# A hybrid decoder layer on one core: other rates for the adaLN columns, pinned sums, later gates, and the mixer's silu by tanh

## The chip, the cores and the metric

The kernel runs on one core of one Trainium2 chip. The metric is the time of one execution in device microseconds (us). Before the change it is 1945.58 us, the median of three runs (1941.93 to 1946.73).

## The reference

One decoder layer of width 2048 for a sequence of 256 rows, in float32. Three residual branches follow one another, each behind an RMSNorm whose shift, scale and gate come from a conditioning vector (adaLN):

```python
cond = jax.nn.silu(c)
mod = cond @ ada_w[l] + ada_b[l]                      # 9 vectors of 2048
sh1, sc1, gt1, sh2, sc2, gt2, sh3, sc3, gt3 = jnp.split(mod, N_MOD, axis=-1)
x = x + 0.5 * gt1 * swiglu(ada_in(x, norm_g[l, 0], sh1, sc1), ...)       # 2048 -> 5632 -> 2048
x = x + gt2 * hybrid_mixer(ada_in(x, norm_g[l, 1], sh2, sc2), ...)
x = x + 0.5 * gt3 * swiglu(ada_in(x, norm_g[l, 2], sh3, sc3), ...)
```

The mixer projects once and runs two groups of eight heads of 128: forgetting attention (causal softmax with a decay from `log_sigmoid`), and a gated delta rule in chunks of 64. The lines of the second group that the change touches:

```python
qkv_g = jax.nn.silu(causal_dwconv(qkv_g, gdn_conv))          # 4 taps
g_log = -jnp.exp(gdn_A_log) * jax.nn.softplus(a_g + gdn_dt_bias)
beta  = jax.nn.sigmoid(b_g)
vb    = v * beta[..., None]
t_inv = triangular_solve(eye + lower, eye, ...)              # 64 x 64 blocks
o_g   = rmsnorm(o_g, gdn_out_norm) * jax.nn.silu(z)
```

## The kernel before

**Weights as one stream.** All matrices together are 5392 tiles of 128 x 128, used in an order fixed at build time, in 674 blocks of 8 tiles. For each block SyncE's queue issues one DMA of 512 KB (`wraw`, L125), ScalarE rounds it to a reduced float32 format (`whi`, L128) and VectorE subtracts to get the rest (`wlo`, L140; below "the split"). TensorE multiplies both parts. There are four buffers of each (a fifth `wraw` is in use in some stretches), so a weight DMA can go when the split four blocks earlier is done. The whole layer is one pass over this stream. By blocks: the first FFN's gate and up products 0 to 112 for its first 28 hidden groups, a first down product 112 to 168, gate and up for the rest 168 to 232 (the "second gate-up"), the second down product 232 to 264; the mixer's projections 264 to 378 and its output projection 378 to 410; the second FFN 410 to 674.

**Columns.** The nine adaLN vectors are computed as 144 columns of 128 values, 16 to a vector. A column takes a DMA of 1 MB (`adat`, L262) and one fused multiply-and-sum of 128 x 2048 on VectorE (L266). `RATE` says how many columns a block starts, from which block on. A sum is issued on VectorE in one of two ways: while `W.late` is set, it is owed and comes behind a split two blocks later (`BEHIND`, `settle`); otherwise it goes into the queue wherever the scheduler puts it. `ada_need` computes columns at once that a residual or norm needs and that aren't there yet. Before, `W.late` is set from the mixer on.

**The mixer's chains.** Projections (steps K, Z, V, F, G of `ORDER`: keys, z rows, values, forgetting heads, gated heads) feed generator chains: gates, decays, keys and solve in the chain "k", and one chain each for gated heads, forgetting heads and outputs. A clock advances by `TILE_US` with each weight tile, and a chain goes on when its last `yield` of so many microseconds has passed; so `yield` sets where in the weight stream the next piece of a chain is placed. `gates` transposes the gate rows (`pcol`, L845), computes softplus and sigmoid on VectorE as a row of small operations on 128 x 48 (L855 to L869), and multiplies by triangles (`prow`, L878). `solve` inverts 16 x 16 blocks for four heads at a time, in 15 dependent steps (L1015, L1016), and moves them through DRAM by DMA (`ld`, `lt`); its result is multiplied into U0 (L1029). Head rows come back from DRAM broadcast (`rowd`, L904 and L929). `conv_silu` takes a projection from PSUM (L955), applies four taps (L959 on ScalarE, L961 on VectorE) and a silu (L962). `gdn` runs a gated head: it transposes q and v (`pvq`, L1056), scales v by beta (`vb`, L1086), and so on. L1204 is the softmax exponential of a forgetting head, `ppt` (L1209) the transpose behind it.

**What sets the order.** Each engine works through its own queue in order. A scheduler writes these queues from the program; `issue_after` holds an instruction back until a given other one is written, of the same queue or another. ScalarE's activations come in sets of functions; the compiler puts an `ACT_TABLE_LOAD` ahead of an activation whose set isn't the loaded one.

Of the kernel before, what the change touches and what calls it, by code (L numbers as in the profile page):

```python
# [12 lines left out]
AF = mybir.ActivationFunctionType  # L13
ALU = mybir.AluOpType
# [18 lines left out]
GR = 24  # L33
NEG = -1e30

RATE = ((0, 0.5), (28, 0.25), (33, 0.5), (49, 0.25), (56, 0.5), (66, 0.2), (90, 0.0), (112, 0.5), (168, 0.45), (232, 0.26), (264, 0.0), (288, 0.295), (384, 0.0), (424, 0.16))
N_BIG, N_GDN = 3, 3
N_FIRST = 2
AHEAD = 4
# [4 lines left out]
LATER = 8  # L44
SLOTS = (3, 11)
BEHIND = 2

HA = 128 + 16
HS = 4 * HA
# [44 lines left out]
class Stream:  # L94


    def __init__(self, nc, w, raw, hi, lo):
        self.nc, self.w, self.raw, self.hi, self.lo = nc, w, raw, hi, lo
        self.order = []
        self.more = None  # L100
        self.h = self.l = self.last = None
        self.owed, self.side, self.quiet = 0.0, lambda: None, False
        self.tc, self.hold, self.held = None, None, []
        self.first = []
        self.lead = None
        self.late, self.owing = False, []

    def settle(self, upto=N_TILES):

# [21 lines left out]
    def next(self, mat, k, n, width=1):  # L131
        i = len(self.order)
        if i % WB == 0:
            nc = self.nc
            b = i // WB
            r, lo = self.first.pop(0) if self.first else self.block(b)
            self.l = lo.tile([P, WB * P], F32R, name="wlo")
            pace = [r_ for r_ in RATE if r_[0] <= b][-1][1]
            with self.behind():
                lo_ = nc.vector.tensor_tensor(self.l, r, self.h.bitcast(F32), ALU.subtract)  # L140
            with self.tc.issue_after(lo_.ins):
                self.settle(b - BEHIND)
            self.split = lo_.ins
            self.owed += 0.0 if self.quiet else pace
            while self.owed >= 1.0:
                self.owed -= 1.0
                self.side()
        for d in range(width):
            self.order.append((mat, k, n, width, d))
        o = (i % WB) * P  # L150
        h, l = self.h[:, o : o + width * P], self.l[:, o : o + width * P]
        return (h, l) if width == 1 else (woven(h), woven(l))
# [3 lines left out]
def layer_kernel(ctx: ExitStack, tc: tile.TileContext, xrow, c, adaw, cols, cst, w, out, order, dbg=None):  # L156
# [597 lines left out]
    def mixer():  # L754
# [76 lines left out]
        def gates(ps):  # L831
# [6 lines left out]
            coef = tiny.tile([P, GR + PAD["hid"]], F32, name="coef", bufs=1)[:, :GR]  # L838
            tc.keep_in_program_order(A.activation(coef, L("alog"), AF.Exp))
            V.tensor_scalar(coef, coef, -1.0, None, ALU.mult)  # L840
            yield 4.0
            pc = psf("pcol")
            pcv = pc[:, : 2 * GR].rearrange("p (t r) -> p t r", t=2)
            for t in range(2):
# [102 lines left out]
        uz = m1p.tile([P, P], F32, name="uz")  # L947
        for t_ in Tms + [Ub, vz, uz]:
            G.memset(t_, 0.0)

        def conv_silu(ps, n, dst, early=None):
            cp, cv = pt("cp"), pt("cv")
            tap = lambda s: L("conv", 4 * n + s, 1)
            if early is None:
                A.copy(runs(cp), turns(ps))  # L955
            else:
                s = early.scaled(cp, ps)
                A.activation(cp, cp, AF.Identity, bias=s)
            A.activation(cv, cp, AF.Copy, scale=tap(3))  # L959
            for d in range(1, 4):  # L960
                V.scalar_tensor_tensor(cv[:, d:], cp[:, : T - d], tap(3 - d), cv[:, d:], ALU.mult, ALU.add)  # L961
            A.activation(dst, cv, AF.Silu)  # L962

        kk = {}

# [23 lines left out]
        def solve(half):  # L989


            hs4, n = slice(4 * half, 4 * half + 4), 2 * NH // 2
            ht = slice(n * half, n * half + n)
            V.tensor_tensor(rb2[:, :, hs4], nbeg[:, :, hs4], r2[:, :, hs4], ALU.mult)
            rk = rsqrt(ssk[:, :, hs4], [P, 2, 4], "k")
            V.tensor_tensor(rkb[:, :, hs4], rk, colS[:, :, 4, hs4], ALU.mult)
            Lh = Ln[:, hs4].rearrange("p h t j -> p (h t) j")
            yield 4.0
            for b in range(8):
                r = slice(16 * b, 16 * b + 16)  # L1000
                with tc.issue_after(W.last):
                    nc.sync.dma_start(ld[ht, b].rearrange("n (r c) -> r n c", r=16), Lh[r, :, r])
                if b % 2:
                    yield 1.4
            yield 3.0
            B = slice(0, 8 * n)
            blk, xt_, pr = (x[B, j] for j in range(4, 7))
            with tc.issue_after(W.last):
                nc.sync.dma_start(blk, ld[ht].rearrange("n b e -> (n b) e"))
            yield 6.0  # L1010
            G.memset(xt_, 0.0)
            G.memset(xt_[:, 0:256:17], 1.0)
            bv, xv, pv = (t_.rearrange("p (i j) -> p i j", i=16) for t_ in (blk, xt_, pr))
            for i in range(1, 16):
                V.tensor_tensor(pv[:, :i, :i], xv[:, :i, :i], bv[:, i, :i].unsqueeze(1).to_broadcast([8 * n, i, i]), ALU.mult)  # L1015
                V.tensor_reduce(xv[:, :i, i], pv[:, :i, :i], mybir.AxisListType.X, ALU.add)  # L1016
                if i % 3 == 0:
                    yield 1.2
            yield 8.0
            with tc.issue_after(W.last):  # L1020
                nc.sync.dma_start(lt[ht].rearrange("n b e -> (n b) e"), xt_)
            yield 3.0
            U = x[:, 7, :P].rearrange("p (n i) -> p n i", n=n)
            with tc.issue_after(W.last):
                nc.sync.dma_start(U, lt[ht].rearrange("n b (q i) -> (b q) n i", q=16))
            yield 5.0
            for q in range(2):
                with tc.issue_after(W.split):
                    V.tensor_tensor(  # L1029
                        U0[:, hs4].rearrange("p h t (b i) -> p (h t) b i", b=4)[:, 4 * q : 4 * q + 4],  # L1030
                        U[:, 4 * q : 4 * q + 4].unsqueeze(2).to_broadcast([P, 4, 4, 16]),
                        C("blk").unsqueeze(1).unsqueeze(3).to_broadcast([P, 4, 4, 16]), ALU.mult)
            if half == 0:
                fetch_rows(1)
            yield 1.0
# [3 lines left out]
        def gdn(h):  # L1039
# [42 lines left out]
            for t in range(2):  # L1082
                sl = slice(t * P, (t + 1) * P)
                j2 = tmp.tile([P, P], BF16, name="j1")
                A.activation(j2, pv[:, T + t * P : T + (t + 1) * P], AF.Square, accum_out=ssq[:, t : t + 1])
                V.tensor_scalar(vb[:, t], pv[:, sl], rkb[:, t, h : h + 1], None, ALU.mult)  # L1086
                A.activation(kb[:, t], kT[:, 1, sl], AF.Copy, scale=rb2[:, t, h : h + 1])
                A.activation(kd[:, t], kT[:, 1, sl], AF.Copy, scale=colS[:, t, 3, h : h + 1])
            V.tensor_scalar(ssq, ssq, EPS, EPS * HD, ALU.add, ALU.mult)
# [156 lines left out]
        def step(kind, h):  # L1246
# [15 lines left out]
            elif kind == "Z":  # L1262
# [5 lines left out]
                pz = project_rows("z", h)  # L1268
                zss[h] = [spare(0), spare(2)] if h else [m1p.tile([P, 512], F32, name=f"zs{t}") for t in range(2)]
                for t in range(2):  # L1270
                    A.activation(zss[h][t], pz[t], AF.Silu)
            elif kind == "V":
                finish("k", NH if h else 0)
                pv = project_rows("vf", h)
# [10 lines left out]
                if h + 1 < NH:  # L1285
                    rowf[h + 1] = row_of(h + 1, 0, "f")

        W.late = True
        first = project([("gt", 0)] + [("qkv", NH + h) for h in range(3)], norm1)
        start("k", -1, gates(first[0]))  # L1290
        for h in range(3):
# [194 lines left out]
```

## Time and profile before

| | |
|---|---|
| median of three runs | 1945.58 us (1941.93 to 1946.73) |
| the profiled execution's own time | 1944.62 us |
| its span, first to last instruction | 1942.8 us |
| mean granted TensorE clock | 0.994 |
| TensorE (PE) busy | 1902.1 us, 98% |
| VectorE (DVE) busy | 1570.4 us, 81% |
| ScalarE (ACT) busy | 1047.1 us, 54% |
| weight splits L140 on VectorE | 674 of 1221 ns, 819.1 us |
| column sums L266 on VectorE | 142 of 2344 ns, 332.9 us |
| DMA, mean of the span | 267 GB/s |

How to read it: the profile is of one execution. A group's row gives source line, engine, operation, output<-inputs with shapes, count, busy us and mean ns of one, and behind the second bar the idle time before these instructions with what ended it. PEld is TensorE's loading of weights, which overlaps its products. A wait's row names the engine and line that waited, the engine and line that released it, total us, how often, and the longest. In a timeline, the number in brackets is the idle time before an instruction and what ended it. A row of windows gives the busy time of each engine in a stretch of time, then the clock granted to TensorE (1.00 is full), the busy share of the DMA engines and GB/s. Idle time on an engine that nobody waits for costs nothing.

### The profile page before, as it was taken

The page shows a single profiled execution, that of the slowest core. Times are in us where ns is not written, and L with a number is a line of the kernel's source. Part 1 is how long each engine was busy: PE and PEld are TensorE (multiplying, and loading weights), DVE is VectorE, ACT ScalarE, POOL GpSimd, SP SyncE. Part 2 cuts the span into 40 slices and gives each one's busy share as a digit, 9 for nine tenths or more (in the row PEclk, how much of TensorE's full clock was granted, in tenths as well). Part 3 has the DMA queues.
Part 4 walks back from the last instruction along what each step waited for, and adds up shares of the span by engine and source line. Part 5 has one row for each costly group of instructions (what it writes and reads, how often), then busy time and mean ns, then how long its engine had stood idle before and what let it go on. Part 6 is the DMA issues. An engine that isn't in the chain of part 4 may idle for free. (4 is left out here: it accounts for less than half of the span.)

```text
span 1942.8 us, 33800 instructions
## 1 busy us (share of the span) xinstructions
PE 1902.1 (98%) x13086; PEld 1774.6 (91%) x13087; DVE 1570.4 (81%) x2455; ACT 1047.1 (54%) x1668; POOL 53.5 (3%) x55
## 2 busy tenths in 40 slices
PE   9999999999999999999999999999999999999998
PEld 7999999988889899888989999999999999999997
DVE  6999978989999999878987989887777665666654
ACT  7444545433444557847656756665554445555553
POOL 0000000000000021000000002000000000000011
PEclk9999999999999999999999999999999999999999
DMA  9988867999999886585677557677777665666663
GB/s 376 354 348 329 325 227 257 399 377 375 365 360 366 327 287 225 199 333 198 207 275 274 204 196 247 203 256 275 263 262 251 227 204 198 203 199 202 200 201 120
DMA packets 129490, 519.58 MB, mean 267 GB/s; under 512 B 18217, under 2 KB 21545, under 8 KB 111153
## 3 DMA queue, kind: packets, MB, share of 16 engines
q1 hardware_dynamic: 129330, 517.42, 74.3%
q8 instruction: 103, 1.69, 0.3%
q14 instruction: 57, 0.47, 0.1%
HBM read 512.89 MB, written 4.47 MB: 266 GB/s over the span
## 5 line engine op out<-in xcount | busy, mean ns | idle before, releaser
L140 DVE TENSOR_TENSOR wlo<-wraw,whi 128x1024 fp32r<-128x1024 f32 x674 | 819.1, 1221 | 264.3 <-ACT whi L128 263.3
L128 ACT CAST whi<-wraw 128x1024 fp32r<-128x1024 f32 x674 | 698.9, 1044 | 523.3 <-PE pd L489 152.9
L489 PE MATMUL pd<-hid,whi 128*128 128x512 f32 x1408 | 461.7, 382 | 0.0
L490 PE MATMUL pd<-hid,wlo 128*128 128x256 f32 x1408 | 384.2, 273 | 2.1 <-DVE wlo L140 2.1
L266 DVE CUSTOM_DVE_ANT_0 adat<-adat,cs,colt 128x2048 f32<-128x2048 f32 x142 | 332.9, 2344 | 7.3 <-DMA adat<-in_ada_dram 7.3
L485 PE MATMUL pg<-hs,whi 128*128 128x512 f32 x912 | 302.7, 382 | 0.5 <-DVE shc L433 0.5
L485 PE MATMUL pu<-hs,whi 128*128 128x512 f32 x912 | 302.4, 382 | 0.0
L489 PEld LDWEIGHTS pd<-hid,whi 128*128 128x128 f32 x1408 | 266.3, 189 | 36.8
L490 PEld LDWEIGHTS pd<-hid,wlo 128*128 128x128 f32 x1408 | 270.3, 192 | 4.0 <-DVE wlo L140 3.9
L486 PE MATMUL pu<-hs,wlo 128*128 128x256 f32 x912 | 249.7, 274 | 5.8 <-DVE wlo L140 5.5
L486 PE MATMUL pg<-hs,wlo 128*128 128x256 f32 x912 | 249.8, 274 | 0.0
L571 PE MATMUL pgu<-hs,wlo 128*128 128x256 f32 x896 | 240.3, 278 | 7.5 <-DVE wlo L140 7.2
L569 PE MATMUL pgu<-hs,whi 128*128 128x256 f32 x896 | 245.0, 277 | 0.4 <-ACT whi L128 0.3
L570 PE MATMUL pgu<-hs,whi 128*128 128x256 f32 x896 | 244.5, 276 | 0.0
L485 PEld LDWEIGHTS pg<-hs,whi 128*128 128x128 f32 x912 | 172.6, 189 | 24.3 <-ACT shc L432 0.7
L485 PEld LDWEIGHTS pu<-hs,whi 128*128 128x128 f32 x912 | 172.6, 189 | 23.4
L486 PEld LDWEIGHTS pu<-hs,wlo 128*128 128x128 f32 x912 | 175.0, 192 | 8.6 <-DVE wlo L140 8.4
L571 PEld LDWEIGHTS pgu<-hs,wlo 128*128 128x128 f32 x896 | 168.6, 193 | 10.5 <-DVE wlo L140 10.4
L486 PEld LDWEIGHTS pg<-hs,wlo 128*128 128x128 f32 x912 | 175.1, 192 | 1.5
L569 PEld LDWEIGHTS pgu<-hs,whi 128*128 128x128 f32 x896 | 172.7, 193 | 1.1 <-ACT whi L128 0.5
L570 PEld LDWEIGHTS pgu<-hs,whi 128*128 128x128 f32 x896 | 172.8, 193 | 0.2 <-DVE hs L383 0.2
L798 PE MATMUL pp<-hs,whi 128*128 128x256 f32 x592 | 170.8, 289 | 0.2 <-ACT whi L128 0.2
(344 smaller groups left out, 2644.9 us busy)
## 6 DMA issues: line engine op xcount, KB each, us to landing
wraw<-in_w_dram SPq DMA_DIRECT2D x674, 512.0 KB, 4.4
adat<-in_ada_dram SPq DMA_DIRECT2D x142, 1024.0 KB, 7.9
xr<-in_xr_dram SPq DMA_DIRECT2D x4, 512.0 KB, 4.9
adaf<-in_ada_dram SPq DMA_DIRECT2D x4, 512.0 KB, 8.2
xd<-x SPq DMA_DIRECT2D x4, 512.0 KB, 7.2
rw<-rowd SPq DMA_DIRECT2D x16, 128.0 KB, 5.5
x<-xd SPq DMA_DIRECT2D x4, 512.0 KB, 5.3
out_dram<-o SPq DMA_DIRECT2D x8, 256.0 KB, 2.8
```

The lines of the kernel that those rows point to most:

```text
L128: self.cast = self.nc.scalar.copy(self.h, r).ins
L140: lo_ = nc.vector.tensor_tensor(self.l, r, self.h.bitcast(F32), ALU.subtract)
L266: V.tensor_tensor_reduce(t, t, cs, 1.0, L("adab", q, 1), ALU.mult, ALU.add, mod[:, q : q + 1])
L485: PE.matmul(ps, wt[0], both, start=(k == 0), stop=False)
L486: PE.matmul(ps[:, T:], wt[1], part(k, HI), start=False, stop=(k == KD - 1))
L489: PE.matmul(ps, wt[0], act.rearrange("p q (a b) -> p q b a", a=2), start=first, stop=False)
L490: PE.matmul(ps[:, :T], wt[1], woven(act[:, 0]), start=False, stop=last)
L569: PE.matmul(o, wh, part(k, HI), start=first and s == 0, stop=False, skip_group_check=skip)
L570: PE.matmul(o, wh, part(k, LO), start=False, stop=False, skip_group_check=skip)
L571: PE.matmul(o, wl, part(k, HI), start=False, stop=last, skip_group_check=skip)
L798: PE.matmul(pp[i][:, :T], wh, hh, start=(k == 0), stop=False)
```

## The change

- `RATE`: 0.2 columns a block hold on from block 66 to 112 (before: to 90, then none to 112); 0.39 in place of 0.45 from 168 to 232, and 0.25 in place of 0.26 to 264.
- `LATE = (66, 112)`: in these blocks too a sum is owed and pinned behind a split; `pinned` takes the place of `late` for the mixer on.
- The gates' `yield` ahead of the transposes is 7 in place of 4. In `solve` the wait ahead of the 15 steps is 8 in place of 6, and the first step is pinned behind the current split.
- `conv_silu`: taps are halved once (so the convolution gives w, half of its argument), ScalarE computes tanh(w), and VectorE (w + w tanh(w)) with one `scalar_tensor_tensor`; that is silu(2w). z is handled alike without halving, which gives twice its silu; the output norm's weights are halved for it.
- `vb` is scaled by ScalarE's copy with a scale in place of VectorE.

Where the order changes, at three places. Line numbers of after are shifted by 2 to 7 (L140 is L142, L266 is L268, L855 is L857, L961 is L965, the new product is L967).

**Second gate-up, VectorE**, from the splits of blocks 178 and 179 on; `tg`, `tu` and `hid` are the products of the hidden groups. Before:

```order
L140 TENSOR_TENSOR wlo<-wraw,whi 128x1024 x2
L497 TENSOR_TENSOR tg<-pg,mg 128x256
L266 ISA adat,mod<-adat,cs,colt 128x2048
L266 ISA mod 128x1
L140 TENSOR_TENSOR wlo<-wraw,whi 128x1024
L497 TENSOR_TENSOR tu<-pu,mg 128x256
L140 TENSOR_TENSOR wlo<-wraw,whi 128x1024
L520 TENSOR_TENSOR tu<-tu,tg 128x256
L504 TENSOR_TENSOR hid<-tu,hid 128x256
L266 ISA adat,mod<-adat,cs,colt 128x2048
L266 ISA mod 128x1
L140 TENSOR_TENSOR wlo<-wraw,whi 128x1024
```

After:

```order
L142 TENSOR_TENSOR wlo<-wraw,whi 128x1024 x2
L499 TENSOR_TENSOR tg<-pg,mg 128x256
L142 TENSOR_TENSOR wlo<-wraw,whi 128x1024
L268 ISA adat,mod<-adat,cs,colt 128x2048
L268 ISA mod 128x1
L499 TENSOR_TENSOR tu<-pu,mg 128x256
L142 TENSOR_TENSOR wlo<-wraw,whi 128x1024
L522 TENSOR_TENSOR tu<-tu,tg 128x256
L142 TENSOR_TENSOR wlo<-wraw,whi 128x1024
L506 TENSOR_TENSOR hid<-tu,hid 128x256
L268 ISA adat,mod<-adat,cs,colt 128x2048
L268 ISA mod 128x1
```

A sum of columns stood behind the splits 179 and 181; it now stands behind 180 and 182. Over blocks 168 to 232 sums are two and three blocks apart in turn; before there were also rows of three that were two apart. Between blocks 66 and 112 sums stand behind the splits 83, 87, 92, 97, 102, 107 and 111, where there were two, at 83 and 109.

**Gates, VectorE**, the softplus chain that ends in the product with `coef`. Before, all of it behind the split of block 278:

```order
L855 TENSOR_SCALAR x<-x 128x48
L856 RECIPROCAL x<-x 128x48
L857 TENSOR_TENSOR x<-x 128x48
L858 TENSOR_TENSOR x<-x 128x48
L859 TENSOR_SCALAR x<-x 128x48
L861 SCALAR_TENSOR_TENSOR x<-x 128x48 x7
L862 SCALAR_TENSOR_TENSOR x<-x 128x48
L867 TENSOR_SCALAR x<-x 128x48
L864 SCALAR_TENSOR_TENSOR x<-x 128x48
L868 RECIPROCAL x<-x 128x48
L865 TENSOR_TENSOR x<-x,coef 128x48
L869 TENSOR_TENSOR colS<-x 128x2x8
```

After, its last part, behind the splits 281, 282 and 283; its first step (L857) is behind split 279:

```order
L863 SCALAR_TENSOR_TENSOR x<-x 128x48
L142 TENSOR_TENSOR wlo<-wraw,whi 128x1024
L863 SCALAR_TENSOR_TENSOR x<-x 128x48
L142 TENSOR_TENSOR wlo<-wraw,whi 128x1024
L863 SCALAR_TENSOR_TENSOR x<-x 128x48
L965 SCALAR_TENSOR_TENSOR cv<-cp,colt,cv 128x255
L864 SCALAR_TENSOR_TENSOR x<-x 128x48
L869 TENSOR_SCALAR x<-x 128x48
L965 SCALAR_TENSOR_TENSOR cv<-cp,colt,cv 128x254
L866 SCALAR_TENSOR_TENSOR x<-x 128x48
L870 RECIPROCAL x<-x 128x48
L867 TENSOR_TENSOR x<-x,coef 128x48
```

The chain was one piece; now splits and the convolutions' operations stand between its steps. On TensorE `pcol` moves from block 275.62 to 275.88 and `prow`, which waits for the chain, from 278.75 to 281.38. Behind it, the rows' first DMA to DRAM (L890) goes from behind the weight DMA of block 283 to that of 288.

**The first heads, ScalarE**, blocks 306 to 308, where forgetting head 0 and gated head 0 begin. Before:

```order
L128 CAST whi<-wraw 128x1024 x3
L955 COPY cp<-pp 128x256
L1204 ACT_TABLE_LOAD
L1204 ACTIVATE x,fzz<-x,fmx 128x128
L1204 ACTIVATE x,fzz<-x,fmx 128x256
L959 ACTIVATE cv<-cp,colt 128x256
L918 ACTIVATE dec<-dec,ng 128x128
L1211 COPY x<-ppt 128x384
L918 ACTIVATE dec<-dec,ng 128x128
L919 ACTIVATE rw<-rw 128x256
L941 ACTIVATE Ln<-Ln,colS 128x128
L962 ACT_TABLE_LOAD
```

After:

```order
L920 ACTIVATE dec<-dec,ng 128x128 x2
L921 ACTIVATE rw<-rw 128x256
L1210 ACTIVATE x,fzz<-x,fmx 128x128
L1210 ACTIVATE x,fzz<-x,fmx 128x256
L959 COPY cp<-pp 128x256
L129 CAST whi<-wraw 128x1024
L963 ACTIVATE cv<-cp,colt 128x256
L129 CAST whi<-wraw 128x1024
L1217 COPY x<-ppt 128x384
L129 CAST whi<-wraw 128x1024
L1227 ACTIVATE j_9857,fss<-pfo 128x128
```

The table loads are gone from this stretch, the decays (`dec`) stand ahead of the exponentials and the weight casts between the single steps. Over the whole program ScalarE has 8 table loads where it had 35. On VectorE the last step of the solve (L1016) stood behind split 298, with a column's sum between; it now stands right behind split 304. U0 (L1029) goes from behind split 302 to behind 307, and `pvq` on TensorE from block 307.0 to 308.5; `ppt` stays at 305.25.

**The same place, SyncE's queue** (`lt` are the solved triangles on their way through DRAM, `rowd` the head rows). Before, from the weight DMAs of blocks 300 and 301 on:

```order
L125 DMA wraw<-in_w_dram 128x1024 x2
L1021 DMA lt<-x 64x256
L904 DMA rw<-rowd 128x256
L125 DMA wraw<-in_w_dram 128x1024
L1025 DMA x<-lt 128x8x16
L262 DMA adat<-in_ada_dram 128x2048
L125 DMA wraw<-in_w_dram 128x1024 x2
L929 DMA x<-rowd 128x4x256
L125 DMA wraw<-in_w_dram 128x1024
L904 DMA rw<-rowd 128x256
L125 DMA wraw<-in_w_dram 128x1024
```

After, from the weight DMAs up to block 305 on:

```order
L264 DMA adat<-in_ada_dram 128x2048
L906 DMA rw<-rowd 128x256
L126 DMA wraw<-in_w_dram 128x1024 x2
L1027 DMA lt<-x 64x256
L126 DMA wraw<-in_w_dram 128x1024
L264 DMA adat<-in_ada_dram 128x2048
L1031 DMA x<-lt 128x8x16
L126 DMA wraw<-in_w_dram 128x1024
L906 DMA rw<-rowd 128x256
L126 DMA wraw<-in_w_dram 128x1024 x2
L931 DMA x<-rowd 128x4x256
L126 DMA wraw<-in_w_dram 128x1024
```

The triangles' DMA stood behind the weight DMA of block 301 and now stands behind that of 307; the rows' DMA (L929, now L931) behind 304 and now behind 311.

```diff
--- before.py
+++ after.py
@@ -33,7 +33,7 @@
 GR = 24
 NEG = -1e30
 
-RATE = ((0, 0.5), (28, 0.25), (33, 0.5), (49, 0.25), (56, 0.5), (66, 0.2), (90, 0.0), (112, 0.5), (168, 0.45), (232, 0.26), (264, 0.0), (288, 0.295), (384, 0.0), (424, 0.16))
+RATE = ((0, 0.5), (28, 0.25), (33, 0.5), (49, 0.25), (56, 0.5), (66, 0.2), (112, 0.5), (168, 0.39), (232, 0.25), (264, 0.0), (288, 0.295), (384, 0.0), (424, 0.16))
 N_BIG, N_GDN = 3, 3
 N_FIRST = 2
 AHEAD = 4
@@ -44,6 +44,7 @@
 LATER = 8
 SLOTS = (3, 11)
 BEHIND = 2
+LATE = (66, 112)
 
 HA = 128 + 16
 HS = 4 * HA
@@ -103,7 +104,7 @@
         self.tc, self.hold, self.held = None, None, []
         self.first = []
         self.lead = None
-        self.late, self.owing = False, []
+        self.late, self.pinned, self.owing = False, False, []
 
     def settle(self, upto=N_TILES):
 
@@ -133,6 +134,7 @@
         if i % WB == 0:
             nc = self.nc
             b = i // WB
+            self.late = self.pinned or LATE[0] <= b < LATE[1]
             r, lo = self.first.pop(0) if self.first else self.block(b)
             self.l = lo.tile([P, WB * P], F32R, name="wlo")
             pace = [r_ for r_ in RATE if r_[0] <= b][-1][1]
@@ -838,7 +840,7 @@
             coef = tiny.tile([P, GR + PAD["hid"]], F32, name="coef", bufs=1)[:, :GR]
             tc.keep_in_program_order(A.activation(coef, L("alog"), AF.Exp))
             V.tensor_scalar(coef, coef, -1.0, None, ALU.mult)
-            yield 4.0
+            yield 7.0
             pc = psf("pcol")
             pcv = pc[:, : 2 * GR].rearrange("p (t r) -> p t r", t=2)
             for t in range(2):
@@ -947,6 +949,8 @@
         uz = m1p.tile([P, P], F32, name="uz")
         for t_ in Tms + [Ub, vz, uz]:
             G.memset(t_, 0.0)
+        for c_ in (L("conv"), L("gdnn")):
+            V.tensor_scalar(c_, c_, 0.5, None, ALU.mult)
 
         def conv_silu(ps, n, dst, early=None):
             cp, cv = pt("cp"), pt("cv")
@@ -959,7 +963,8 @@
             A.activation(cv, cp, AF.Copy, scale=tap(3))
             for d in range(1, 4):
                 V.scalar_tensor_tensor(cv[:, d:], cp[:, : T - d], tap(3 - d), cv[:, d:], ALU.mult, ALU.add)
-            A.activation(dst, cv, AF.Silu)
+            A.activation(cp, cv, AF.Tanh)
+            V.scalar_tensor_tensor(dst, cp, 1.0, cv, ALU.add, ALU.mult)
 
         kk = {}
 
@@ -1007,12 +1012,13 @@
             blk, xt_, pr = (x[B, j] for j in range(4, 7))
             with tc.issue_after(W.last):
                 nc.sync.dma_start(blk, ld[ht].rearrange("n b e -> (n b) e"))
-            yield 6.0
+            yield 8.0
             G.memset(xt_, 0.0)
             G.memset(xt_[:, 0:256:17], 1.0)
             bv, xv, pv = (t_.rearrange("p (i j) -> p i j", i=16) for t_ in (blk, xt_, pr))
             for i in range(1, 16):
-                V.tensor_tensor(pv[:, :i, :i], xv[:, :i, :i], bv[:, i, :i].unsqueeze(1).to_broadcast([8 * n, i, i]), ALU.mult)
+                with tc.issue_after(W.split) if i == 1 else nullcontext():
+                    V.tensor_tensor(pv[:, :i, :i], xv[:, :i, :i], bv[:, i, :i].unsqueeze(1).to_broadcast([8 * n, i, i]), ALU.mult)
                 V.tensor_reduce(xv[:, :i, i], pv[:, :i, :i], mybir.AxisListType.X, ALU.add)
                 if i % 3 == 0:
                     yield 1.2
@@ -1083,7 +1089,7 @@
                 sl = slice(t * P, (t + 1) * P)
                 j2 = tmp.tile([P, P], BF16, name="j1")
                 A.activation(j2, pv[:, T + t * P : T + (t + 1) * P], AF.Square, accum_out=ssq[:, t : t + 1])
-                V.tensor_scalar(vb[:, t], pv[:, sl], rkb[:, t, h : h + 1], None, ALU.mult)
+                A.activation(vb[:, t], pv[:, sl], AF.Copy, scale=rkb[:, t, h : h + 1])
                 A.activation(kb[:, t], kT[:, 1, sl], AF.Copy, scale=rb2[:, t, h : h + 1])
                 A.activation(kd[:, t], kT[:, 1, sl], AF.Copy, scale=colS[:, t, 3, h : h + 1])
             V.tensor_scalar(ssq, ssq, EPS, EPS * HD, ALU.add, ALU.mult)
@@ -1268,7 +1274,8 @@
                 pz = project_rows("z", h)
                 zss[h] = [spare(0), spare(2)] if h else [m1p.tile([P, 512], F32, name=f"zs{t}") for t in range(2)]
                 for t in range(2):
-                    A.activation(zss[h][t], pz[t], AF.Silu)
+                    A.activation(zss[h][t], pz[t], AF.Tanh, scale=0.5)
+                    V.scalar_tensor_tensor(zss[h][t], zss[h][t], 1.0, pz[t], ALU.add, ALU.mult)
             elif kind == "V":
                 finish("k", NH if h else 0)
                 pv = project_rows("vf", h)
@@ -1285,7 +1292,7 @@
                 if h + 1 < NH:
                     rowf[h + 1] = row_of(h + 1, 0, "f")
 
-        W.late = True
+        W.late = W.pinned = True
         first = project([("gt", 0)] + [("qkv", NH + h) for h in range(3)], norm1)
         start("k", -1, gates(first[0]))
         for h in range(3):
```

## The prediction

> **What bounds the kernel now.** I read the page's busy times first, then the waits of TensorE (PE), then windows stage by stage, and last the timeline around the longest waits.
>
> ```profile
> PE 1902.1 (98%) x13086; PEld 1774.6 (91%) x13087; DVE 1570.4 (81%) x2455; ACT 1047.1 (54%) x1668; POOL 53.5 (3%) x55
> L140 DVE TENSOR_TENSOR wlo<-wraw,whi 128x1024 fp32r<-128x1024 f32 x674 | 819.1, 1221 | 264.3 <-ACT whi L128 263.3
> L266 DVE CUSTOM_DVE_ANT_0 adat<-adat,cs,colt 128x2048 f32<-128x2048 f32 x142 | 332.9, 2344 | 7.3 <-DMA adat<-in_ada_dram 7.3
> ```
>
> TensorE is busy for 1902.1 of 1942.8 us, and no matmul is added or removed. The change can therefore only move its waits: 40.7 us idle, plus what waits hide inside busy time (slow clock, late weight loads). Which waits those are:
>
> ```profile
> PE pu L486 <- DVE wlo L140: 5.5, 3, 2.0
> PE pvq L1056 <- ACT qv L962: 3.4, 3, 2.9
> PE ppt L1209 <- ACT x L1204: 2.3, 2, 2.2
> PE pd L490 <- DVE wlo L140: 2.1, 6, 0.6
> PE pcol L845 <- ACT x L836: 1.6, 1, 1.6
> PE pp L800 <- DVE wlo L140: 0.8, 1, 0.8
> PE prow L878 <- DVE x L865: 0.6, 1, 0.6
> PEld pu L486 <- DVE wlo L140: 8.1, 8, 2.3
> ```
>
> Columns: total us, times, longest; the last row is for 480 to 657 us alone. The stages, as windows (start:end, length, busy of PE, PEld, DVE, ACT, POOL, then the granted clock, the DMA share and GB/s):
>
> ```profile
> 206.00:261.00 55.00, 55.00 (x495) 55.00 (x494) 49.41 (x74) 31.32 (x44) 0.00 (x0) 1.00 0.81 295
> 261.00:284.00 23.00, 23.00 (x209) 23.00 (x208) 16.01 (x23) 11.04 (x16) 0.00 (x0) 1.00 0.65 205
> 284.00:329.00 45.00, 45.00 (x406) 45.00 (x405) 36.58 (x63) 25.09 (x40) 0.00 (x0) 1.00 0.69 230
> 480.00:657.00 177.00, 171.28 (x1028) 154.47 (x1027) 163.49 (x189) 83.22 (x124) 0.00 (x0) 1.00 0.96 363
> 657.00:740.00 83.00, 82.97 (x507) 76.10 (x506) 81.53 (x122) 46.62 (x68) 15.13 (x13) 1.00 0.83 294
> 860.00:900.00 40.00, 33.73 (x267) 32.65 (x267) 31.50 (x67) 26.90 (x62) 0.42 (x2) 0.91 0.63 236
> 900.00:930.00 30.00, 28.03 (x245) 27.33 (x245) 27.94 (x90) 23.32 (x61) 0.00 (x0) 1.00 0.62 215
> 930.00:960.00 30.00, 29.24 (x257) 28.67 (x257) 29.47 (x99) 20.93 (x51) 0.00 (x0) 1.00 0.68 239
> ```
>
> Three places lose time that this change touches: the second gate-up (480 to 657), the gates, and the first heads (860 to 900).
>
> **Columns.** In the second gate-up a tile takes two matmuls, so 1028 are 64.25 blocks of 8 tiles. The stretch behind it runs nearly without waits: 507 matmuls, 31.7 blocks, 83.0 us, 2.62 us a block. At that pace 64.25 blocks take 168.3 us, and the window took 177: 8.7 us lost. VectorE (DVE) has 163.49 us of work there, 2.54 a block against TensorE's 2.62, so any bunch of sums makes the split late. One case:
>
> ```profile
> 520.11 2.35 DVE L266 CUSTOM_DVE_ANT_0 adat<-adat,cs,colt 128x2048 f32<-128x2048 f32 x1
> 522.38 1.22 DVE L140 TENSOR_TENSOR wlo<-wraw,whi 128x1024 fp32r<-128x1024 f32 x1
> 523.66 0.38 PE L486 MATMUL pu<-hs,wlo 128*128 128x256 f32 x1 [1.77 <-DVE wlo L140]
> ```
>
> The sum stands ahead of the split for which TensorE waits. Rate 0.45 gives 28.8 sums in these 64 blocks, 0.39 gives 25: four fewer are 4 x 2.34 = 9.4 us off DVE, which leaves 154.1 us, 2.40 a block. The order shows gaps of 2 and 3 blocks in turn, no longer several twos running. I take -6: the three long waits (5.5) and a little; at most all 8.7 go; +1 if the gain is only moved.
>
> The sums are not gone: about five more come between blocks 66 and 112, pinned behind a split. They cost 11.7 us of DVE, against 5.6 + 7.0 + 8.4 = 21 us idle in the first three windows, where TensorE is never idle. What they use up is the lead with which DVE enters the down product, where TensorE's waits on splits are 2.1 in all. I take +0.7, from 0 to +2.1 (as many again). Their DMAs, 5 MB more there, meet a share of 0.65 to 0.81. The tail of the columns keeps its total.
>
> **The silu.** tanh stays with the exponentials; the order shows 27 table loads fewer on ScalarE (ACT), all in the mixer.
>
> ```profile
> L962 ACT ACT_TABLE_LOAD x14 | 18.0, 1283 | 1.2 <-DVE cv L961 0.9
> L1204 ACT ACT_TABLE_LOAD x4 | 5.1, 1283 | 0.1
> L1086 DVE TENSOR_SCALAR vb<-pvq,rkb x16: 341/345/352, 886.9 to 1133.7; 128x128 f32<-128x128 f32 x16
> L961 DVE SCALAR_TENSOR_TENSOR cv<-cp,colt,cv x72: 465/477/485, 772.5 to 1120.8; 128x255 f32<-128x255 f32 x24, 128x254 f32<-128x254 f32 x24, 128x253 f32<-128x253 f32 x24
> L1271 ACT ACTIVATE zs<-pv x2: 598/598/599, 824.2 to 824.8; 128x512 f32<-128x512 f32 x2
> ```
>
> ACT gets 27 x 1.283 = 34.6 us less. DVE gets 24 x 0.477 = 11.4 us more for the convolutions, 4 products of 512 columns at 0.48 to 0.95 each (one to two times the row; 0.7 taken, 2.8 together), and 16 x 0.345 = 5.5 us less for vb: +8.7. What the loads are worth is only what TensorE waits for. The longest such waits:
>
> ```profile
> 868.03 1.28 ACT L1204 ACT_TABLE_LOAD   x1
> 869.88 0.33 PE L1209 MATMUL ppt<-colt,x 128*128 128x128 f32 x1 [2.18 <-ACT x L1204]
> 878.71 1.28 ACT L962 ACT_TABLE_LOAD   x1
> 880.01 0.42 ACT L962 ACTIVATE qv<-cv 128x256 f32<-128x256 f32 x1
> 880.48 0.47 PE L1056 MATMUL pvq<-colt,qv 128*128 128x128 f32 x1 [2.92 <-ACT qv L962]
> ```
>
> In both the load stands directly before the awaited activation and covers 1.28 us of the wait. The clock is 0.91 over these 40 us, which costs 3.6 us, in the stretch that holds these two waits; I take it that they cause it.
>
> The Trainium skill, TensorE: Matmul & The Clock Gate, Part 1: The HAM clock gate, puts the fall to half clock behind an idle window of about 3.4 us. Both waits here are shorter, 2.18 and 2.92; if only a whole such window of idleness counts, something else slowed the clock, the 3.6 us stay, and the sum below would be -6.3 instead of -9.9.
>
> The Trainium skill, ScalarE: Activation LUTs, What ACT_TABLE_LOAD costs, adds a drain of 1.38 us to each load, 2.66 us a switch. By it ACT would gain 71.8 us, and 1.4 us more of pvq's wait would go: -11.3. The trace disagrees: the load of 878.71 ends at 879.99 and the activation starts at 880.01, so the sum goes by 34.6.
>
> **The later gates.** SyncE's queue was blocked twice just before these waits (its waits between 830 and 870 us):
>
> ```profile
> SPq L1021 <- DVE x L1016: 4.3, 1, 4.3
> SPq L929 <- DVE U L1029: 2.6, 1, 2.6
> SPq L929 <- DMA x<-lt: 2.5, 1, 2.5
> ```
>
> Weight DMAs stand behind the one of the solved triangles (L1021) and the one of head rows (L929), and were held 9.4 us in all; that ate the lead of the splits before 860. In the order of before, the solve's last step stands behind split 298 with a sum (2.34) ahead of it; now it stands right behind split 304, when the weight DMA behind the triangles is due anyway. The rows' DMA waited for the product of L1029, behind split 302, with the next weight due since split 301; now that product is behind split 307 and the next weight is due with 308. So both holds should shrink to about a microsecond, and the splits keep their lead.
>
> For 860 to 900 I count waits of 2.3 + 2.9 + 0.8 and 3.6 of clock, 9.6 us. I take -7.5: pvq still waits 2.1 of its 2.9 for convolution, tanh and the new product. Bounds -9.6 and -3 (one wait, no clock).
>
> The gates pay. Their softplus chain on DVE now stands behind five splits and more convolutions:
>
> ```profile
> 785.64 0.19 DVE L855 TENSOR_SCALAR x<-x 128x48 f32<-128x48 f32 x1 [1.62 <-ACT x L850]
> 789.49 0.14 DVE L865 TENSOR_TENSOR x<-x,coef 128x48 f32<-128x48 f32 x1
> 789.68 0.39 PE L878 MATMUL prow<-cstt,x 128*8 128x128 f32 x2 [0.60 <-DVE x L865]
> ```
>
> By the order DVE has 5 splits (6.1) and about 12 products of 0.48 (5.7) more before the last step, 11.8 us, less the 1.62 waited now; prow moves from PE block 278.75 to 281.38, 2.63 blocks of 2.62, 6.9 us. So prow would wait 0.6 + 11.8 - 1.6 - 6.9 = 3.9, of which the table loads ahead of this chain's own exponentials give some back (1.28 each): I take a wait of 3, against 0.6, less 0.5 at pcol: +2. Bounds: -2.2 (both present waits go) and +5 (3.3 more of wait, and 1.8 of clock, half of that at 860). Queued behind the chain on DVE are splits, so TensorE's next blocks may wait too; that is in the upper end. The z columns hold their banks for a tanh (0.60) and a product (0.7) each instead of one activation, so the value projection behind them may start 0.9 later (a product and some queueing; 0 to +2).
>
> **The rest of the mixer.** A head's two convolutions give DVE +0.95 and vb -0.69: +0.26 a head, 1.8 for seven heads, if DVE decides; its 29.47 of 30 at 930 says it nearly does. Against it stand TensorE's 2.0 and 0.8 us idle at 900 and 930. I take 0, from -3 to +3. The halving of constants (two small DVE operations) lies at the head of the queue at the start, where DVE waits for ScalarE anyway: 0, at most 0.4 if that cover is gone. Second FFN and output projection keep their order: 0.
>
> Sum: -6 + 0.7 - 7.5 + 2 + 0.9 + 0 = -9.9. Span 1942.8 becomes 1932.9. The profiled execution's own time was 1944.62, 1.8 above its span: 1934.7. The median of the three runs, 1945.58, stands 1.0 above that: 1935.7, so 1936.
>
> **The rivals.** About 0.3% of 1945.58, 5.8 us, is what a measurement of this kernel can tell from no change; the bounds are 1939.7 and 1951.4.
>
> (a) The waits only change their name. In the heads DVE is at 27.94 and 29.47 of 30, and qv now takes one DVE product more; freed ACT then does not help, and 860 to 900 gives -3 instead of -7.5. With gates at +3.5 and the second gate-up at -5, the sum is -2.9 (0.7 and 0.9 included): 1942.7, no change. For it: DVE's shares; against: the table loads stand directly in the two waits. Chance 0.16.
>
> (b) Slower: the softplus chain decides. If DVE reaches prow more than about 3 us late, that is as long as the wait at 880 that went with a slow clock, the clock halves, the gate rows come late, and with them the decays and the first heads, which wait again. Price: 3.8 and 3.6 of clock at the gates, and the 9.6 at 860 not saved but met again with 3.6 more of clock; with -4 at the gate-up and the 0.7 and 0.9: 7.4 + 3.6 - 4 + 1.6 = +8.6, 1954. For it: DVE's load at the gates; against: in the new order the rows are fetched four blocks later anyway, and each halt of TensorE lets DVE catch up. Chance 0.13.
>
> (c) All of it pays: second gate-up -8.7, first heads -9.6, gates 0, rest -3, and +0.7: -20.6, 1925. For it: DVE at 2.40 a block leaves 0.2 a block. Chance 0.15.
>
> (d) The transfers bind in the second gate-up (DMA share 0.96), so fewer sums give nothing: -9.9 + 6 = -3.9, 1941.7. Against it: each sum removed takes 1 MB along, and TensorE waits there for the split. Chance 0.04, with no change.
>
> **How the numbers follow.** My forecast near 1936, from which the sum may miss by 4, has 0.52; (c) 0.15; together with 0.02 of small mixtures, faster has 0.69. No change is (a) and (d), 0.20 less what of them falls below the bound: 0.18. Slower: 0.13. The range leaves out the far half of (c) and most of (b): 1925 to 1947.
>
> **What would show it.** Right: three long waits of pu L486 (now L488) gone, DVE near 154 of 177 in the second gate-up; pd waits in the first down product up to 4 us; 8 table loads instead of 35; 860 to 900 with clock 1.00 and neither ppt nor pvq above 2 us; SyncE not waiting 4 us at the triangles' DMA; prow waiting 2 to 4 us on its DVE chain. Wrong: a clock under 1.00 around 790 or 880, splits late at 900 to 1000, or the pu waits still there.

## The result, and the profile after

The changed kernel takes 1940.08 us in the median of 14 runs (1936.37 to 1944.37), against 1945.16 us for the kernel before in the 14 runs beside it (1941.93 to 1948.65). The ratio is 0.9976, with a 95% interval of 0.9969 to 0.9984: 0.24% faster, which is clear of the scatter of so many runs but below the 0.3% that the prediction drew as the line for "faster". The time lies in the range (1925 to 1947); the forecast of 1936 asked for twice the gain. The profiled execution took 1940.15 us, with a span of 1938.3.

The engines' busy times, from the page after the change:

```profile
PE 1898.7 (98%) x13086; PEld 1772.7 (91%) x13087; DVE 1573.7 (81%) x2469; ACT 1018.3 (53%) x1657; POOL 53.9 (3%) x55
```

ScalarE lost 28.8 us of work, VectorE gained 3.3, TensorE has the same 13086 products. The longest waits of TensorE after:

```profile
PE pgu L573 <- DVE wlo L142: 16.3, 13, 2.7
PE pd L492 <- DVE wlo L142: 2.3, 7, 0.6
PE pvq L1062 <- DVE qv L967: 1.8, 2, 1.5
PE pcol L847 <- ACT x L838: 1.6, 1, 1.6
...
PE prow L880 <- DVE x L867: 0.6, 1, 0.6
...
PE pv L816 <- DVE zs L1278: 0.5, 1, 0.5
```

The waits of `pu` in the second gate-up and of `ppt` are gone from the list, and that of `pvq` is about halved. In their place stands `pgu`, the first gate and up products, with 16.3 us. Before, it was 7.2:

```profile
PE pgu L571 <- DVE wlo L140: 7.2, 8, 2.7
```

The stages, as windows of the profile after:

```profile
206.00:261.00 55.00, 55.00 (x495) 55.00 (x495) 48.00 (x72) 29.66 (x42) 0.00 (x0) 1.00 0.78 284
261.00:284.00 23.00, 22.10 (x198) 21.91 (x197) 15.28 (x20) 9.91 (x13) 0.00 (x0) 1.00 0.76 272
284.00:329.00 45.00, 39.40 (x348) 38.83 (x348) 34.59 (x57) 21.83 (x33) 0.00 (x0) 1.00 0.68 232
...
480.00:657.00 177.00, 176.30 (x1067) 160.50 (x1066) 161.61 (x189) 85.91 (x125) 0.00 (x0) 1.00 0.95 357
...
860.00:900.00 40.00, 38.34 (x337) 37.83 (x336) 35.77 (x78) 24.82 (x67) 0.42 (x2) 1.00 0.79 273
```

TensorE idled nowhere between 206 and 329 us before; now it idles 6.5 us there. Between 480 and 657 it idles 0.7 us (before 5.7), between 860 and 900 1.7 (before 6.3), and there the clock is 1.00.

Windows cut at fixed times mix a gain with the shift that it makes. So here is the time of stretches of blocks, from the start of the first product with a low part of one block to that of the other, in one profiled execution of each:

```
blocks         what                              before   after    difference
66 to 112      first gate-up, 0.2 a block        123.27   135.36   +12.1
112 to 168     first down product                150.43   151.02    +0.6
168 to 232     second gate-up                    177.11   169.32    -7.8
275 to 290     gates, keys, first z rows          47.89    47.93     0.0
290 to 298     values                             21.32    21.45    +0.1
298 to 310     first forgetting and gated heads   47.85    38.39    -9.5
310 to 410     other heads, output projection    341.77   340.20    -1.6
410 to 674     second FFN                        707.04   708.49    +1.5
```

They add up to -4.6; the spans differ by 4.5. The +1.5 in the second FFN belongs to no step of the change. It comes with one wait of 1.2 us of `pd` for a hidden group; of the six kernels below with the same rates of columns there or nearly so, one shows a like wait (708.7 us), the other five took 707.0 to 707.6.

### The profile page after: what moved, and what is told of

Read it like the earlier page. It is cut to its first block, busy times and chain, and to the rows that moved or that the text cites. A ratio compares the mean times of both kernels' runs of the same rounds, so it can differ in the third digit from the quotient of the medians.

```text
span 1938.3 us, 33825 instructions
## 1 busy us (share of the span) xinstructions
PE 1898.7 (98%) x13086; PEld 1772.7 (91%) x13087; DVE 1573.7 (81%) x2469; ACT 1018.3 (53%) x1657; POOL 53.9 (3%) x55
## 4 chain that ended last, share of the span: by engine, by line
PE 75%; DVE 13%; issue 4%; DMA 4%; ACT 2%; SPq 0%; DVEq 0%; ACTq 0%
PE pd L491 14%; PE pg L487 10%; PE pu L487 10%; PE pd L492 7%; PE pg L488 5%; PE pu L488 5%; DVE wlo L142 5%; DMA adat<-in_ada_dram 3%; PE po L491 3%; PE pgu L573 3%; PE pgu L571 2%; PE pgu L572 2%; DVE adat L268 2%; PE pp L800 2%; PE pp L801 2%
## 5 line engine op out<-in xcount | busy, mean ns | idle before, releaser
L142 DVE TENSOR_TENSOR wlo<-wraw,whi 128x1024 fp32r<-128x1024 f32 x674 | 818.9, 1221 | 256.3 <-ACT whi L129 254.7
L268 DVE CUSTOM_DVE_ANT_0 adat<-adat,cs,colt 128x2048 f32<-128x2048 f32 x142 | 332.9, 2345 | 20.2 <-DMA adat<-in_ada_dram 20.2
L573 PE MATMUL pgu<-hs,wlo 128*128 128x256 f32 x896 | 241.5, 280 | 16.7 <-DVE wlo L142 16.3
```

Of the source, the lines that this page charges most:

```text
L268: V.tensor_tensor_reduce(t, t, cs, 1.0, L("adab", q, 1), ALU.mult, ALU.add, mod[:, q : q + 1])
L573: PE.matmul(o, wl, part(k, HI), start=False, stop=last, skip_group_check=skip)
```

## Where the 12 us of the first gate-up went

VectorE's waits for columns between 205 and 348 us, before:

```profile
DVE adat L266 <- DMA adat<-in_ada_dram: 1.3, 3, 0.7
```

and after:

```profile
DVE adat L268 <- DMA adat<-in_ada_dram: 18.5, 7, 3.9
```

The sums themselves are 2.35 us each as ever. But VectorE stands in front of them until their DMA has landed, and the next split waits behind. One case, on SyncE's queue:

```profile
289.62 0.43 SPq L264 DMA_DIRECT2D adat<-in_ada_dram  x1
```

on VectorE:

```profile
292.79 1.22 DVE L142 TENSOR_TENSOR wlo<-wraw,whi 128x1024 fp32r<-128x1024 f32 x1 [0.52 <-ACT whi L129]
297.96 2.35 DVE L268 CUSTOM_DVE_ANT_0 adat<-adat,cs,colt 128x2048 f32<-128x2048 f32 x1 [3.94 <-DMA adat<-in_ada_dram]
...
300.90 1.22 DVE L142 TENSOR_TENSOR wlo<-wraw,whi 128x1024 fp32r<-128x1024 f32 x1
```

and on TensorE:

```profile
302.18 0.38 PE L573 MATMUL pgu<-hs,wlo 128*128 128x256 f32 x1 [2.26 <-DVE wlo L142]
```

The column's DMA is issued at 289.62, behind the weight DMA of block 100, and has landed 8.3 us later. VectorE has done split 97 at 294.0 and comes to the sum 4 us early. Splits 97 and 98 end 8.1 us apart; TensorE takes 2.68 us for a block. The first such sums (behind 78, 83 and 87; both kernels also have sums behind 70, 74 and 78, which the list of the order leaves out) ate the lead of the splits (how long before TensorE begins a block its split is done), which fell from 5.3 us at block 78 to 0.05 at block 88. From then on each cost TensorE a wait, of 0.9, 1.7, 2.3, 1.6 and 2.6 us, and the last, at 333.7, also slowed the clock by 1.7 us. That is 10.8 of the 12.1 us; the other 1.3 us show as no wait and stay unexplained.

Why is the sum so early, when it should be pinned behind a later split? In the order of the changed kernel the DMAs behind weight blocks 90, 95, 100, 105 and 110 belong to the sums behind splits 87, 92, 97, 102 and 107: each sum stands three blocks ahead of the place at which its DMA is issued. The code says why: `gate_up_first` calls `ada_need` for each of its products, and `ada_need` ends with `W.settle()`, which places every owed sum at once, without the pin. With `LATE = (0, 0)`, no pin at all, the order of the program is word for word that of the changed kernel on TensorE, VectorE, ScalarE and SyncE. So the pin does nothing in blocks 66 to 112.

## The experiments

**The pin made to hold.** `ada_need` settles early only if the column asked for is itself still owed (or in the mixer):

```diff
-            W.owing.append((len(W.order) // WB, total))
+            W.owing.append((len(W.order) // WB, total, i))
...
-        W.settle()
+        if W.pinned or any(o[2] <= ada_seq.index((m, j)) for o in W.owing):
+            W.settle()
```

> The changed kernel, but while the first FFN's gate and up products run an owed sum is settled only when its column is needed or two blocks have passed, so that the pin holds: sums stand behind split 92, 97, 102, 107 instead of 87, 92, 97, 102, their DMAs stay where they were. Theory (the column's DMA is late: VectorE stood 15.1 us at five sums for their DMA, with splits queued behind): blocks 80 to 112 take what they took before the change (85.8 us instead of 97.9), VectorE's wait for these DMAs falls below 1 us, and the time is about 12 us below the changed kernel, near 1928. Rival (VectorE's own work, 11.7 us of sums more, is what eats the lead): the work is the same, so the time stays within 2 us of 1940 and TensorE still waits for splits there.

Measured: 1933.65 us, ratio to before 0.9944 (0.9931 to 0.9956). Blocks 66 to 112 take 123.27 us, to the hundredth what they took before, with five columns more loaded and four more sums (the fifth stands behind split 112). But blocks 112 to 140 take 80.3 instead of 73.4. There a sum still stands ahead of its DMA, and another one follows. VectorE of this kernel:

```profile
328.82 2.35 DVE L268 CUSTOM_DVE_ANT_0 adat<-adat,cs,colt 128x2048 f32<-128x2048 f32 x1 [1.18 <-DMA adat<-in_ada_dram]
...
335.27 2.35 DVE L268 CUSTOM_DVE_ANT_0 adat<-adat,cs,colt 128x2048 f32<-128x2048 f32 x1
```

The pin ends at block 112, so the column of block 113, unpinned, goes behind split 111, two blocks ahead of its DMA, and the pinned one of 110 comes behind 112. TensorE then waits 3.01 us and runs 6.8 us at half clock. In blocks 66 to 112 the theory holds; the expected time was missed by that new bunch. How much of it is the late DMA is another matter: VectorE stood 1.18 us for it, so without it TensorE would still have waited some 1.8 us for split 113 (an estimate from these two numbers), behind two sums in neighbouring blocks.

**Pins kept to block 120.** Same edit, and

```diff
-LATE = (66, 112)
+LATE = (66, 120)
```

> As the kernel with real pins (realpin), with the pins kept to block 120. realpin won all of blocks 80 to 112 but lost 6.9 us in 112 to 140, where a sum stood behind split 111 and waited 1.2 us for its DMA, and another behind 112. Now the sums stand behind 112, 115, 117, 119, all two blocks behind their DMA. Theory (a sum placed ahead of its DMA's landing is what costs): blocks 112 to 140 return to within 1.5 us of the 73.4 of before, and the time falls to about 1927 to 1929. Rival (the lead is used up by sums and hidden groups that end together at 112): the loss stays above 4 us, time near 1933.

Measured: 1927.58 us, ratio 0.9910 (0.9897 to 0.9924). Blocks 112 to 140 take 73.38 us. This is the fastest kernel of the study, 0.9% below before and 12.5 us below the changed kernel. Its windows:

```profile
261.00:284.00 23.00, 23.00 (x209) 23.00 (x208) 19.62 (x27) 10.96 (x15) 0.00 (x0) 1.00 0.77 271
284.00:329.00 45.00, 45.00 (x406) 45.00 (x405) 41.61 (x69) 25.38 (x40) 0.00 (x0) 1.00 0.80 276
```

VectorE is busier than in the changed kernel (41.61 against 34.59 of 45 us) and TensorE does not wait: the work of the sums fits, as the prediction had counted. What did not fit was the time for which VectorE stood still.

**Pins to 120, and no column from block 106 to 112.**

```diff
-(66, 0.2), (112, 0.5)
+(66, 0.2), (106, 0.0), (112, 0.5)
```

> As pinlong, and no column is started between block 106 and 112, so no sum stands behind split 112 (sums behind 107, 115, 117, 119). Theory: blocks 112 to 140 at 73.4, time 1926.5 to 1928. Rival of pinlong: here too the loss goes, so that pinlong and this one differ by over 3 us if the bunch at 112 is the cause, and by under 1 us if the late DMA was.

Measured: 1929.27 us (0.9914, 0.9901 to 0.9928), a little above what was expected; blocks 112 to 140 again 73.36. The two kernels are not told apart by their times, and both lose nothing there, so a sum behind split 112 does no harm by itself. What caused the 6.9 us with the pins to 112 they don't separate, against what was expected of them: in both, the column of block 113 went from split 111 to split 115, which took away its wait and the neighbouring sum at once. The kernel of the next experiment, without the DMAs of these columns, again has that sum behind 111, with a wait of 0.3 us, but none behind 112, and loses 0.5 us there; so the bunch seems to weigh more than the wait, which is read off and not shown.

**The same sums without their DMA.** In the changed kernel, the columns started in 66 to 112 (nine, one more than the expectation says) load nothing and run over the tile of the column before. From split 87 on they stand at the places they had; the first four stand one to three blocks earlier (behind 67, 72, 77 and 82 instead of 70, 74, 78 and 83):

```diff
+        elif LATE[0] <= len(W.order) // WB < LATE[1] and not W.pinned:
+            t = ada_st["t"]
         else:
             t = (adap if W.more is None or i % 3 else W.more).tile([P, D], F32, name="adat")
...
+            z_ = LATE[0] <= (len(W.order) - 1) // WB < LATE[1] and not W.pinned
+            with tc.issue_after(W.splits[(len(W.order) - 1) // WB - 3]) if z_ else ...
```

> The changed kernel, but the eight columns started in blocks 66 to 112 load nothing: their sums run over the tile of the column before, at the places of the changed kernel (behind splits 87, 92, 97, 102, 107, 111). It leaves out the loading of these eight columns. The sums' work on VectorE and their place ahead of the next split are unchanged. Theory (VectorE stands waiting for the column's DMA): blocks 80 to 112 at 85.8 us as before the change, time near 1928. Rival (a sum of 2.3 us in that place delays the split whatever it waits for): the loss of about 12 us stays, time near 1940.

Measured: 1930.25 us (0.9927, 0.9910 to 0.9943), and blocks 80 to 112 at 85.75 us, as before the change. VectorE's wait for columns there:

```profile
DVE adat L274 <- DMA adat<-in_ada_dram: 0.3, 1, 0.3
```

The same sums from split 87 on, no wait, no loss. Loading was taken away here and not only the wait for it; but the kernels with a pin that holds load all these columns, place the sums later, and lose nothing in blocks 66 to 112 either. Together this settles the cause of the 12 us: sums placed ahead of their DMA, not VectorE's work and not the traffic.

**The mixer's changes alone** (the changed kernel with the rates of before):

> The changed kernel with the old rates and no pin (the mixer's changes alone). If the parts add, as the block times of the two profiles say (12.1 us lost in blocks 80 to 112, 7.8 us won in 168 to 232, 8.8 won in the mixer), this gives 1945.2 - 8.8 = 1936.4, faster than the changed kernel by about 4 us. Rival (the mixer's gain hangs on where the columns stand there): 1940 or more.

Measured: 1936.42 us (0.9956, 0.9943 to 0.9968), as the sum said.

**The columns alone** (the kernel before with the new rates and the pin):

> The kernel before with the changed kernel's rates and its pin alone; silu, v and yields as before. By the block times: 12.1 lost in 80 to 112 and 7.8 won in 168 to 232, so 4.3 us slower than before, about 1949.5. Rival (the columns shift the mixer's heads, as the 2.0 us in blocks 304 to 310 between the changed kernel and the one with the old rates hint): also 2 us won there, 1947.5.

Measured: 1943.03 us, 0.9995 (0.9986 to 1.0005): no difference, and a miss of both theories, 6.5 and 4.5 us under what they said. Blocks 66 to 112 lost 11.2 us and 168 to 232 won 7.8, as expected. But blocks 298 to 310 won 5.2 too, though nothing of the mixer's code was changed.

**The tanh alone:**

> The kernel before with the silu by tanh alone; old rates, old yields, v still scaled by VectorE. Theory of the prediction (the table loads stood in the two waits, 1.28 us each, and these waits halved the clock for 3.6 us): 4 to 6 us faster than before, about 1940, clock near 1.00 between 860 and 900, while SyncE still waits over 4 us at the solved triangles. Rival (the later gates carry the gain, since the splits had lost their lead through SyncE's queue): at most 2 us faster.

Measured: 1938.38 us (0.9964, 0.9950 to 0.9977), more than the theory gave. Yet the wait of `ppt`, from which the table load was taken away, got longer:

```profile
869.16 1.18 PE L1213 MATMUL ppt<-colt,x 128*128 128x128 f32 x3 [3.09 <-ACT x L1208]
```

It was 2.18 us before, and now slows the clock as well (0.61 over the next 4 us). The wait of `pvq` fell from 2.92 to 0.9.

**The later gates alone:**

> The kernel before with the later gates, the later solve and its pinned first step alone. Theory of the prediction: SyncE's holds at the triangles' and the rows' DMAs shrink, so blocks 298 to 304 lose 1 to 2 us of waits, the gates cost up to 2 us, and the table loads' waits of blocks 304 to 310 mostly stay: within 3 us of before. Rival (later gates carry the gain): 6 us faster or more, with blocks 304 to 310 at 22 to 24 us instead of 29.6.

Measured: 1938.82 us (0.9964, 0.9952 to 0.9977). The theory's "within 3 us" falls; the rival has the gain right, but blocks 304 to 310 take 25.9 us, not 22 to 24.

**v scaled by VectorE again** (in the changed kernel):

> The changed kernel with v scaled by VectorE again: 16 x 0.345 us on VectorE more, 16 x 0.395 on ScalarE less. If VectorE sets the pace of the heads (busy 29.4 of 30 us at 900 and 930): 1 to 3 us slower than the changed kernel, in blocks 304 to 378. If not: within 1 us.

Measured: 1939.71 us (0.9976, 0.9966 to 0.9986) against 1940.08: no difference. Who scales v doesn't matter here.

**What the three single changes share.** Blocks 298 to 310 took 47.9 us before, 43.8 with the tanh alone, 42.6 with the later gates alone, 42.7 with the columns alone, 38.4 with all. Three unrelated edits each win 4 to 5 us in the same place, and they don't add. The lead of the split over TensorE, as TensorE begins a block, in us:

```
block            293   295   297   299   301   303   305   307   309
before           0.1   0.2   0.8   0.3   3.4   0.1   1.0   0.5   0.6
columns alone    3.0   3.5   3.1   1.8   1.7   3.7   3.8   4.0   3.0
tanh alone       5.3   3.8   4.1   2.8   4.9   3.0   3.8   6.8   6.0
later gates      4.3   4.6   0.9   0.9   2.0   1.2   2.6   2.7   0.1
changed kernel   5.5   5.4   5.5   4.3   4.4   4.4   5.0   5.6   8.3
```

Before, the splits entered the first heads with no lead, and each small delay there reached TensorE. Any of the edits moves sums, solve steps or activations among the splits and leaves a lead. In the order of before, 15 dependent operations of the solve stand in one piece between splits 292 and 293; in the others that piece comes later or is broken up. The traces bear that out. In the order of before VectorE first stands 1.2 us for the DMA that brings the solve its blocks (`ld`), the piece takes 3.1 us and the next split 1.2, while TensorE takes 2.6 for a block: the lead falls from 2.4 us at block 292 to 0.1 at 293. With the later gates the same piece stands behind split 296, the wait is 2.5 us, and the lead falls from 5.0 to 0.9. But neither the piece nor its wait was taken away by itself, so the cause stays open.

## Why the prediction was right and where it was wrong

- **Second gate-up: right in mechanism, under-sized.** -6 forecast, -7.8 measured. Four sums fewer and gaps of two and three in turn removed all three waits of `pu`, not just the long part of them; VectorE's windows row reads 161.61 of 177, in a window that now begins some five blocks earlier in the program.
- **Columns in 66 to 112: the step that failed.** "I take +0.7, from 0 to +2.1" measured +12.1, with 0.6 more in the down product. The working compared 11.7 us of sums with 21 us of idle VectorE, and the experiments confirm that part: the work fits. It took the pin from the code as it was meant ("pinned behind a split") and asked of the DMAs only whether there was bandwidth (share 0.65 to 0.81), not when each is issued against the place of its sum. SyncE's queue and VectorE's, laid side by side by blocks, would have shown each sum three blocks ahead of its DMA, and the trace of before had a small case of it, 0.7 us at the sum behind split 83. Nothing in the list of rivals had this wait.
- **Gates: the price didn't come.** +2 forecast, 0.0 measured; `prow` waits 0.6 us, as before, not 3. The error was to add all new work on VectorE to the old end of the softplus chain. VectorE was 3 to 5 us ahead of TensorE at these blocks in the changed kernel, so the splits between the chain's steps were early work, not delay; this is read from the trace and was not tried. It also took some luck: in the kernel that scales v on VectorE, where the gates' code is the same, the clock fell behind the 1.63 us wait of `pcol`, and these blocks took 49.5 us.
- **z rows: right in kind, over-sized.** +0.9 forecast, +0.1 measured in the value projection, `pv` waits 0.5 us for its product. That product takes 0.68 us, the 0.7 assumed.
- **First heads: right in sum, not in its reasons.** -7.5 forecast for blocks around 860 to 900, -9.5 measured in 298 to 310. The wait of `ppt` vanished in the whole, but the tanh alone made it longer; the table load inside a wait was not what the wait was worth. And the gain varies: in the five kernels above with the changed kernel's mixer (the three with a pin that holds, the one without the DMAs, the one with the old rates) blocks 298 to 310 took 38.6 to 41.8 us. In three of them a wait of 1.7 to 2.3 us slowed the clock again, in one (no column from block 106 to 112) that of `ppt`, back at 2.17 us. SyncE's holds at the triangles' and the rows' DMAs were to shrink to about 1 us each, from 4.3 and 5.1. They are still 3.9 and 3.3:

```profile
SPq L1027 <- DVE x L1022: 3.9, 1, 3.9
...
SPq L931 <- DVE cv L965: 2.9, 1, 2.9
SPq L931 <- DMA x<-lt: 0.4, 1, 0.4
```

  and TensorE doesn't wait, because the splits have a lead of 4 to 5 us when it comes. The clock's 3.6 us came back as forecast.
- **Table loads and v:** 8 loads are left, as counted. The rest of the mixer came out at -1.6 against 0 (-3 to +3). The new product takes 0.42 us, not the 0.48 of the nearest row.
- **Rival (c)**, near 1925, "all of it pays": with a pin that holds, and holds to block 120, the same changes give 1927.6. The changed kernel was kept from this by a pin that did nothing.

That the total came near was luck: two misses of opposite sign met. 12 us were lost where under 1 was counted, and some 8 us were won beyond the forecast in the gates, the second gate-up, the heads and the rest of the mixer together.

## What to carry to other kernels

When work that needs a transfer is moved, lay the queue that issues the transfer and the queue that uses it side by side, and read for each pair how far the use stands behind the issue; spare time of the engine and bandwidth of the DMAs say nothing about that. A pin or a rule in the source should be seen in the order before it is believed: here leaving it out changed no instruction. And where an in-order engine runs ahead of the bound one, read its lead block by block: here a hold of 3.9 us cost nothing where the lead was 4 to 5 us, and three unrelated edits each won 4 to 5 us in the one place that had no lead.

## What the runs showed of the hardware

TensorE's clock fell to half after waits well under 3 us. In the eleven profiles of this case (two kernels and nine experiments), every single wait of 2.50 us or more (2.50, 2.60, 2.64, eleven of 2.72, 2.92, 3.01, 3.09) was followed by 4 us at a mean clock of 0.50 to 0.66. Of waits between 2.0 and 2.5 us five were (2.02, 2.17, 2.27, 2.27, 2.42) and three were not (2.18, 2.26, 2.44). Of 36 waits from 1.37 to 2.0 us two were (1.63, 1.74). The changed kernel, after its waits of 2.26 and 2.60 us:

```profile
302.20:306.20 4.00, 4.00 (x36) 4.00 (x37) 3.99 (x7) 2.78 (x4) 0.00 (x0) 1.00 0.66 190
333.70:337.70 4.00, 3.97 (x24) 3.97 (x25) 4.00 (x8) 2.89 (x5) 0.00 (x0) 0.66 0.76 276
```

In the clock's records of these traces, the half clock lasted 3.41 us in 22 of these 24 cases, which is 1.7 us lost, and 6.83 us in two, after the waits of 2.92 and 3.01 us, which is 3.4. So a wait of 2 to 2.5 us may cost 1.7 us more than it lasts, and one of 2.5 us or more cost at least that each time. In the first heads of before it was the 2.92 us of `pvq` alone that slowed the clock; the 2.18 us of `ppt`, named along with it in the prediction, did not. The Trainium skill, TensorE: Matmul & The Clock Gate, Part 1: The HAM clock gate, gives an idle window of about 3.4 us for the fall to half clock; no wait here was that long, so the trace disagrees with taking that as the least wait that matters.
